# Making the first MLP weight operands during the in-projection: one step per token tile behind its norm, loads behind the projection's weights, sums on VectorE

## The chip, the cores and the metric

One core of one Trainium2 chip runs the kernel. The metric is the device time of one execution in microseconds. The engines are named as in the profile: PE (TensorE, matrix products), PEld (its weight loads), DVE (VectorE), ACT (ScalarE), POOL (GpSimd) and SP (SyncE, which issues almost all the DMAs here).

## The reference

One layer of an encoder with two kinds of attention in parallel, in float32, for 1024 and 256 tokens with the same weights. Cut to what matters here:

```python
n = rms_norm(h, g_mix)
z = n @ w_in                                   # qa, ka, va | qb, kb, vb
qb = axial_rope(rms_norm(qb, g_qnorm))         # per head of 64
kb = axial_rope(rms_norm(kb, g_knorm))
oa = diff_attention(qa, ka, va); ob = gqa_attention(qb, kb, vb)
h = h + concat(oa, ob) @ w_out
h = h + relu(rms_norm(h, g_mlp) @ w_ff1) ** 2 @ w_ff2
h = h + sigmoid(rms_norm(h, g_ple) @ w_gate) * (p @ w_proj)
y = rms_norm(h, g_final)
```

## The kernel before

All 1280 tokens are worked on together, as ten tiles of 128. A float32 product is made of three products of a high and a low part (`hi*hi + hi*lo + lo*hi`), so every operand is split first: ACT copies it to the rounded high part, DVE or POOL subtracts that from the operand to get the low part. The MLP uses a seven-product scheme of the Strassen kind on 2x2 blocks, so its weights are needed as sums and differences of four blocks `a11, a12, a21, a22`, each split, named by numbers 1 to 7.

The program has these stages: in-projection (0 to about 215 us), attention woven with the last projection units and the output projection (to about 800 us), the two MLP products (to about 1600 us), then gate and output.

The in-projection goes by units. A `b_unit` makes 256 columns of q (or k and v) of mixer B: for each token tile 24 matmuls into a PSUM bank `psb`, then `norm_rope`, a chain of small operations that normalises and rotates each head: `sq` (ACT, squares), `zg` and `ss` (DVE, scaled copy and sum of squares), `rq4v` (DVE), `rq4u` and `rr` (ACT, logarithm and exponential), three small `rq4u` steps and `rr` (DVE), `ra` (POOL, twice) beside `rb` (DVE, twice), and at last `ro` (DVE). Two token tiles later PE transposes `ro` into `trb`, ACT and DVE split that into `qkl`, and it is written to DRAM. A `va_unit` makes 256 columns of v: 24 matmuls per tile into `psv`, split into `vl`, written to DRAM as `vad`. `weave` alternates groups of matmuls of two units: units b0 and va1 from about 68 to 140 us, then b1 and `qk_a` (the first q and k of mixer A, banks `psa`, split into `zl`) to about 206 us. PSUM banks and the tiles `vl`, `w1o` and `xt` come in pairs.

Beside these units `early_w1` makes the split MLP weights of the first two groups of 256 columns of `w_ff1`: it loads two 512 KB blocks per group into the slots Q0 and Q1 (`w1e`), scales them by `gmlp` on ACT (eight 128x256 operations), makes four sums on POOL (`w1t`, lines 473, 474, 479, 480), splits the seven operands (`w1o`: ACT line 466, DVE line 467) and writes each to DRAM (`wed`, 512 KB). It is a generator; `along` takes one step of it after every fourth group of matmuls of the b unit, that is once per token tile. The slots Q0 and Q1 are used again for the first `kt` and `qt` of the attention, and the two buffers of `w1o` are those of `xt`.

The order of the instructions on each engine is set by a scheduler when the program is built: it takes the code in the order written and moves instructions by its own estimate of times. `tc.issue_after(x)` keeps every instruction of the block behind `x` on x's engine. All loads that go through `load` are chained in the order of the code, on SP's queue. Each engine carries out its instructions strictly in that order, so an instruction that waits holds up everything behind it.

Of the kernel before, what the change touches and what calls it, by code (L numbers as in the profile page):

```python
# [14 lines left out]
F32 = mybir.dt.float32  # L15
F32R = mybir.dt.float32r
F16 = mybir.dt.float16
AF = mybir.ActivationFunctionType
ALU = mybir.AluOpType
# [4 lines left out]
P = 128  # L24
# [16 lines left out]
def f(ap):  # L41
    return ap.bitcast(F32)
# [3 lines left out]
def encoder_kernel(ctx: ExitStack, tc: tile.TileContext, x, xT, pT, w_in, w_out, w_ff1, w_ff2, w_gate, w_proj,  # L46
# [38 lines left out]
    V, S, G, PE = nc.vector, nc.scalar, nc.gpsimd, nc.tensor  # L85
    dma = nc.sync.dma_start
# [3 lines left out]
    def load(*args):  # L90

        with tc.issue_after(chain[-1].ins) if chain else contextlib.nullcontext():
            chain[:] = [dma(*args)]
        return chain[0]
# [65 lines left out]
    RAWB = 6  # L160
    EVERY = 4
    FETCH = ((4, 6), (5, 7), (6, 2), (8, 5))

    def load_w(src, cols, n, rawp, wp, tag, lo_eng, between={}, dma=dma):

        c0 = cols
        hi, lo = [], []
        kn = 512 // n
        kw = {"bufs": WHB} if n == 256 else {}
        for kk in range(KD // kn):  # L170
            if kk in between:
                between[kk]()
            raw = rawp.tile([P, kn, n], F32, tag="raw", name=f"raw{tag}", bufs=RAWB if n == 256 else 2)
            w_dma[:] = [dma(raw, src[kk * kn * P:(kk + 1) * kn * P, c0:c0 + n].rearrange("(k p) c -> p k c", p=P))]
            a = wp.tile([P, kn, n], F32R, tag="wh", name=f"wh{tag}", **kw)
            b = wp.tile([P, kn, n], F32R, tag="wl", name=f"wl{tag}", **kw)
            S.activation(a, raw, AF.Copy)
            lo_eng.tensor_tensor(b, raw, f(a[:]), op=ALU.subtract)
            hi += [a[:, i, :] for i in range(kn)]
            lo += [b[:, i, :] for i in range(kn)]  # L180
        return hi, lo
# [4 lines left out]
    def slot(tag, shape, dt, name):  # L186
        return slot_pool[tag].tile(shape, dt, tag=tag, name=name, bufs=1)
# [25 lines left out]
    def pj(name):  # L213
        return ppj.tile([P, 512], F32, tag="pj", name=name)

    def weave(main, side, ratio, stop=False):


        owed = 0.0
        for c in main:  # L220
            owed += c * ratio
            while owed > 0 and side is not None:
                d = next(side, None)
                if d is None:
                    side = None
                    if stop:
                        return
                    break
                if d == 0.0:
                    break  # L230
                owed -= d
        if side is not None:
            drain(side)

    def drain(gen):
        for _ in gen:
            pass
# [28 lines left out]
    def tok_pairs(w, t):  # L266
        wh, wl = w
        c = slice(t * P, (t + 1) * P)
        pr = []
        for k in range(KD):  # L270
            pr += [(xh[:, k, c], wh[k]), (xh[:, k, c], wl[k]), (xl[:, k, c], wh[k])]
        return pr
# [4 lines left out]
    gq = bp.tile([P, 64], F32, name="gq", bufs=1)  # L277
    gk = bp.tile([P, 64], F32, name="gk", bufs=1)

    def norm_rope(ps, t, nh, g):  # L280
        r1 = rstd1[:, t:t + 1]
        sq = bp.tile([P, 4, 64], F32, tag="sq", name="sq")
        zg = bp.tile([P, 4, 64], F32, tag="zg", name="zg")
        ps3 = ps[:, :nh * 64].rearrange("p (h d) -> p h d", d=64)
        S.activation(sq[:, :nh], ps3, AF.Square, scale=r1)
        V.scalar_tensor_tensor(zg[:, :nh], ps3, r1, g[:, None, :].to_broadcast([P, nh, 64]),
                               op0=ALU.mult, op1=ALU.mult)
        ss = bp.tile([P, 4], F32, tag="ss", name="ss")
        V.tensor_reduce(out=ss[:, :nh], in_=sq[:, :nh], axis=AX.X, op=ALU.add)
        rr = bp.tile([P, 4], F32, tag="rr", name="rr")  # L290
        rsqrt(rr[:, :nh], ss[:, :nh], 1.0 / 64, 1e-6, bp, nh, f"rq{nh}")
        a = bp.tile([P, 4, 64], F32, tag="ra", name="ra")
        b = bp.tile([P, 4, 64], F32, tag="rb", name="rb")
        G.tensor_tensor(a[:, :nh], zg[:, :nh], rc[:, t:t + 1, :].to_broadcast([P, nh, 64]), op=ALU.mult)
        z4 = zg[:, :nh].rearrange("p h (a b e) -> p h a b e", a=2, b=2)
        b4 = b[:, :nh].rearrange("p h (a b e) -> p h a b e", a=2, b=2)
        s4 = rs[:, t, :].rearrange("p (a b e) -> p a b e", a=2, b=2)
        for q in range(2):
            V.tensor_tensor(b4[:, :, :, q, :], z4[:, :, :, 1 - q, :],
                            s4[:, None, :, q, :].to_broadcast([P, nh, 2, 16]), op=ALU.mult)  # L300
        G.tensor_tensor(a[:, :nh], a[:, :nh], b[:, :nh], op=ALU.add)
        o = bp.tile([P, 4, 64], F32, tag="ro", name="ro", bufs=3)
        V.tensor_tensor(o[:, :nh], a[:, :nh], rr[:, :nh, None].to_broadcast([P, nh, 64]), op=ALU.mult)
        return o.rearrange("p h d -> p (h d)")

    def b_unit(u, w, hook=None):
# [55 lines left out]
    def va_unit(u, w):  # L362
        for t in range(NT):
            ps = pj("psv")
            yield from mm_gen(ps[:, :256], tok_pairs(w, t))
            hl = bp.tile([P, 2, 2, P], F32R, tag="vl", name="vl")
            v3 = ps[:, :256].rearrange("p (h d) -> p h d", d=P)
            r1 = rstd1[:, t:t + 1]
            S.activation(hl[:, :, 0, :], v3, AF.Copy, scale=r1)
            V.scalar_tensor_tensor(hl[:, :, 1, :], v3, r1, f(hl[:, :, 0, :]), op0=ALU.mult, op1=ALU.subtract)  # L370
            for j in range(2):
                dma(vad[2 * u + j][t * P:(t + 1) * P], f(hl[:, j]))
# [16 lines left out]
    def qk_a(h):  # L389

        for c, dst, sc in ((512 + P * h, kd[h], 1.0), (P * h, qd[h], -0.125 / SLOPES[h])):
            w = load_w(w_in, c, P, rawp, wp, "a", G, dma=load)
            yield from qk_unit(dst, sc, w)

    def wload(c, between={}, dma=dma):
        return load_w(w_in, c, 256, bp, bp, "p", V, between, dma)
# [27 lines left out]
    w_b0, w_va1 = wload(1536, dma=load), wload(1280, dma=load)  # L424
# [26 lines left out]

    def early_w1():
        for p in range(NEW):
            raws = []
            for kh in range(2):
                raw = slot(f"Q{kh}", [P, 4, 256], F32, "w1e")
                load(raw, w_ff1[kh * 512:kh * 512 + 512, p * 256:(p + 1) * 256].rearrange("(k p) c -> p k c", p=P))
                for k in range(4):
                    S.activation(raw[:, k], raw[:, k], AF.Copy, scale=gmlp[:, 4 * kh + k:4 * kh + k + 1])
                raws.append(raw)  # L460
            a11, a12, a21, a22 = (raws[x][:, :, c * P:c * P + P] for c in range(2) for x in range(2))
            yield

            def out(i, src):
                hl = bp.tile([P, 2, 4, P], F32R, tag="xt", name="w1o", bufs=2)
                S.activation(hl[:, 0], src, AF.Copy)
                V.tensor_tensor(hl[:, 1], src, f(hl[:, 0]), op=ALU.subtract)
                dma(wed[p, i], f(hl[:]))

            out(1, a11)  # L470
            t = bp.tile([P, 2, 4, P], F32, tag="qkl", name="w1t", bufs=1)
            s3, s2 = t[:, 0], t[:, 1]
            G.tensor_tensor(s3, a11, a21, op=ALU.subtract)
            G.tensor_tensor(s2, a22, s3, op=ALU.subtract)
            yield
            for i, src in ((6, s2), (7, s3), (2, a12)):
                out(i, src)
                yield
            G.tensor_tensor(s3, a12, s2, op=ALU.subtract)
            G.tensor_tensor(s2, a21, a22, op=ALU.add)  # L480
            for i, src in ((5, s2), (4, a22), (3, s3)):
                out(i, src)
                yield

    def along(main, side, every):

        for n, c in enumerate(main):
            yield c
            if n % every == every - 1:
                next(side, None)  # L490

    early = early_w1()
    weave(along(b_unit(0, w_b0), early, EVERY), va_unit(1, w_va1), 1.0)
    weave(along(b_unit(1, wload(1792, dma=load)), early, EVERY), qk_a(0), 1.0)
    drain(early)
    bs.close()

# [256 lines left out]
    for h in range(4):  # L754
# [6 lines left out]
        ends = (bl[6], al[4], bl[7]) if h == 3 else (bl[6], bl[7], al[4])  # L761
# [245 lines left out]
    side = side_work()  # L1007
# [182 lines left out]
    for n, c in enumerate(side):  # L1190
        flush()
        for m, i in FETCH:
            if len(op_done) >= m and i not in WN[0]:
# [329 lines left out]
    for ti, t in enumerate(FORD):  # L1523
# [19 lines left out]
        ends = []  # L1543
# [62 lines left out]
        for n0 in range(0, 512 if last else D, 512):  # L1606
            n = slice(n0, n0 + 512)
# [54 lines left out]
```

## Time and profile before

| | |
|---|---|
| median of 3 runs | 1719.1 us (1718.8 to 1721.23) |
| the profiled execution | 1720.6 us; its span from first to last instruction 1718.7 us |
| PE busy | 1669.3 us, 97% of the span, so 49.4 us in which PE had nothing running |
| DVE, ACT, POOL busy | 69%, 51%, 39% |
| DMA | mean 162 GB/s over the span; above 300 GB/s in the first 40 us |
| mean granted TensorE clock | 0.996 of full speed |

A row of the timeline gives start, duration, engine, line, operation and tiles, and in brackets the idle time of the engine just before it and what ended that. A row of the windows gives the busy time of each engine in a stretch, then the granted TensorE clock, the DMA share and GB/s. A row of the waits gives who waited for whom: total in us, times, longest.

### The profile page before, as it was taken

To read this page: it belongs to the slowest core of one execution; us is meant where nothing else is said; L and a number is where in the kernel's file an instruction comes from. 1 tells how busy PE (TensorE), PEld (TensorE's weight loads), DVE (VectorE), ACT (ScalarE), POOL (GpSimd) and SP (SyncE) were. 2 spreads that over 40 slices of the span, in tenths; PEclk is the share of its full clock that TensorE was granted. 3 is DMA by queue.
4 is the path that set the end of the run, shared out by engine and by line. 5 is a ranking of instruction groups with operands and counts; after the bars stand their busy time and mean duration, and the time that the engine had idled before them with its cause. 6 is when DMAs were issued, how large, how long until landed. Compare 5 with 4: busy or idle time off the path is not lost.

```text
span 1718.7 us, 27284 instructions
## 1 busy us (share of the span) xinstructions
PE 1669.3 (97%) x9849; PEld 1490.0 (87%) x9849; DVE 1183.8 (69%) x2107; ACT 868.4 (51%) x1749; POOL 673.4 (39%) x659
## 2 busy tenths in 40 slices
PE   8979999999999999999999999999999999999997
PEld 8979888888878888889999999998888888888886
DVE  7777678878878878668666665665665855355666
ACT  8543268767866667675332333333433333354644
POOL 1153445635754435333556665620433400001441
PEclk9999999999999999999999999999999999999999
DMA  9774493432773534395433343449666456532111
GB/s 311 240 255 154 158 236 111 124 121 87 216 204 110 155 99 124 110 314 193 157 126 137 129 151 123 136 162 386 213 219 200 127 192 201 167 121 69 45 44 50
DMA packets 191867, 278.28 MB, mean 162 GB/s; under 512 B 13674, under 2 KB 121076, under 8 KB 191732
## 3 DMA queue, kind: packets, MB, share of 16 engines
q1 hardware_dynamic: 189988, 271.28, 49.3%
q0 software_dynamic: 1600, 5.24, 1.0%
q8 instruction: 78, 1.28, 0.3%
q14 instruction: 57, 0.47, 0.1%
q10 hardware_dynamic: 144, 0.00, 0.0%
HBM read 182.63 MB, written 88.61 MB: 158 GB/s over the span
## 4 chain that ended last, share of the span: by engine, by line
PE 76%; DVE 8%; DMA 6%; ACT 4%; issue 3%; POOL 2%; SPq 1%; POOLq 0%; ACTq 0%; DVEq 0%
PE psa L242 6%; PE pso L242 5%; PE sc L621 5%; PE av L699 5%; PE tr L675 4%; PE psb L242 2%; PE psg L1553 2%; DMA vad<-vl 1%; DVE pl L686 1%; DMA xt<-in_x 1%; PE psv L242 1%; PE f__16296 L156 1%; PE f__15256 L156 1%; PE f__16638 L156 1%; PE f__15601 L156 1%
## 5 line engine op out<-in xcount | busy, mean ns | idle before, releaser
L1350 ACT ACTIVATE ao<-ar 128x1280 fp32r<-128x1280 f32 x56 | 71.3, 1275 | 189.4 <-PE f__16300 L156 37.8
L621 PE MATMUL sc<-kt,qt 128*128 128x512 f32 (+1 forms) x576 | 156.1, 391 | 7.7 <-ACT p L646 5.0
L686 DVE TENSOR_TENSOR pl<-tr,ph 128x512 fp32r<-128x512 f32 x204 | 138.1, 685 | 33.2 <-ACT ph L681 32.0
L1352 DVE TENSOR_TENSOR ao<-ar,ao 128x1280 fp32r<-128x1280 f32 x56 | 93.3, 1666 | 89.0 <-ACT ao L1350 89.0
L681 ACT ACTIVATE ph<-tr 128x512 fp32r<-128x512 f32 x204 | 120.0, 596 | 56.8 <-PE tr L675 50.0
L242 PE MATMUL pso<-ow,mt 128*128 128x512 f32 x480 | 119.3, 395 | 3.5 <-DVE osq L726 1.3
L675 PE MATMUL tr<-ident,p 128*128 128x128 f32 x768 | 115.6, 273 | 6.4 <-DVE pl L686 5.7
L621 PEld LDWEIGHTS sc<-kt,qt 128*128 128x128 f32 x576 | 98.9, 189 | 26.1 <-ACT p L646 6.5
L1553 PE MATMUL psg<-gw,n 128*128 128x512 f32 (+1 forms) x504 | 115.4, 384 | 0.0
L675 PEld LDWEIGHTS tr<-ident,p 128*128 128x128 f32 x768 | 91.4, 140 | 22.8 <-DVE pl L686 9.2
L1553 PEld LDWEIGHTS psg<-gw,n 128*128 128x128 f32 x504 | 90.8, 188 | 19.5
L1071 POOL TENSOR_SCALAR w1r<-w1r,gmlp 128x256 f32<-128x256 f32 x112 | 79.2, 726 | 69.1 <-DMA w1r<-in_w_ff 48.3
L242 PEld LDWEIGHTS pso<-ow,mt 128*128 128x128 f32 x480 | 87.4, 188 | 21.6 <-DVE osq L726 2.0
L699 PE MATMUL av<-ph,vt 128*128 128x256 f32 x544 | 102.3, 289 | 0.9 <-DVE osq L726 0.4
L660 POOL TENSOR_SCALAR p<-p,rl 128x1024 f32<-128x1024 f32 x64 | 75.1, 1176 | 51.0 <-DVE rl L658 48.4
L1144 ACT ACTIVATE w<-w1s 128x512 fp32r<-128x512 f32 x56 | 35.2, 628 | 116.4 <-POOL w1s L1151 54.4
L638 DVE TENSOR_REDUCE mm<-sc 128x1 f32<-128x1024 f32 (+1 forms) x80 | 84.2, 1056 | 8.8 <-PE sc L621 8.3
L699 PE MATMUL av<-pl,vt 128*128 128x256 f32 x408 | 89.6, 301 | 0.0
L699 PEld LDWEIGHTS av<-ph,vt 128*128 128x128 f32 x544 | 82.3, 190 | 6.3 <-DVE osq L726 1.2
L646 ACT ACTIVATE p<-sc,mm 128x1024 f32<-128x1024 f32 x64 | 71.4, 1115 | 25.5 <-DVE mm L638 16.7
L634 DVE CUSTOM_DVE_ANT_0 p<-sc,dist 128x1024 f32<-128x1024 f32 x64 | 77.6, 1219 | 8.3 <-PE sc L621 4.4
L643 ACT ACTIVATE p<-p,mm 128x1024 f32<-128x1024 f32 x64 | 73.5, 1149 | 18.0 <-DVE mm L634 17.2
(1520 smaller groups left out, 4748.8 us busy)
## 6 DMA issues: line engine op xcount, KB each, us to landing
ar<-ad SPq DMA_DIRECT2D x56, 640.0 KB, 4.1
w2r<-in_w_ff SPq DMA_DIRECT2D x56, 512.0 KB, 4.6
qt<-qd SPq DMA_DIRECT2D x160, 128.0 KB, 3.0
ad<-q SPq DMA_DIRECT2D x64, 320.0 KB, 2.8
ad<-qs SPq DMA_DIRECT2D x48, 320.0 KB, 2.2
w1r<-in_w_ff SPq DMA_DIRECT2D x28, 512.0 KB, 4.4
md<-ml SPq DMA_DIRECT2D x40, 256.0 KB, 2.2
mt<-md SPq DMA_DIRECT2D x20, 512.0 KB, 6.3
```

Of the source, the lines that this page charges most:

```text
L242: PE.matmul(ps, a, b, start=i == 0, stop=i == n - 1)
L621: PE.matmul(ps[:, h0:h0 + n], shared["q"][:, cc, v, i * P:(i + 1) * P], kt[:, s0 + h0:s0 + h0 + n], start=v == 0, stop=v == 1)
L634: V.tensor_tensor_reduce(out=p[:, :sn], in0=ps[:, :sn], in1=dst_t[:, off:off + sn], scale=SLOPES[idx], scalar=3.0e38, op0=ALU.add, op1=ALU ...
L638: V.tensor_reduce(out=st["m", i][:, 0:1], in_=ps[:, :sn], axis=AX.X, op=ALU.max, negate=True)
L660: G.tensor_scalar(p[:, :sn], p[:, :sn], rl[:, 0:1], 1.0, op0=ALU.mult, op1=ALU.mult)
L675: PE.transpose(t[:, jj, i * P:(i + 1) * P], st["ws"][i][:, j * P:(j + 1) * P], ident)
L681: S.activation(ph, st["tr", j2], AF.Copy)
L686: V.tensor_tensor(pl, st["tr", j2], f(st["ph", j2][:]), op=ALU.subtract)
L699: PE.matmul(st["av"][:, :256], x_, y_, start=j2 == 0 and n == 0, stop=j2 == nj - 1 and n == len(pr) - 1)
L1071: G.tensor_scalar(raw[:, k], raw[:, k], gmlp[:, 4 * kh + k:4 * kh + k + 1], 1.0, op0=ALU.mult, op1=ALU.mult)
L1352: V.tensor_tensor(ao[:, 1], a, f(ao[:, 0]), op=ALU.subtract)
L1553: ends[:] = [PE.matmul(ps, a, b, start=m == 0, stop=m == len(pr) - 1)]
```

## The change

Four things are changed in the in-projection, none elsewhere.

- The steps of `early_w1` start later in each unit: none in the first eight groups of matmuls of unit b0 (`SKIP`), none in the first four of b1 (`SKIP2`); before there was a step in every fourth group from the start.
- Each step is kept behind the first (ACT, `sq`) and the last instruction (DVE, `ro`) of the norm that was written last, on those two engines (`rope_ends`).
- Both loads of a group now make a step of their own, and the eight scalings the next one: nine steps per group instead of eight. There are 8 + 9 places for 18 steps, the last step is taken after both units. In the code the loads of the second group now come behind the weights of unit b1 and `qk_a`.
- The four sums of each group (`w1t`) are made on DVE instead of POOL.

```diff
+    SKIP = 8
+    SKIP2 = 4
...
+    rope_ends = []
...
-        S.activation(sq[:, :nh], ps3, AF.Square, scale=r1)
+        ends = [S.activation(sq[:, :nh], ps3, AF.Square, scale=r1)]
...
-        V.tensor_tensor(o[:, :nh], a[:, :nh], rr[:, :nh, None].to_broadcast([P, nh, 64]), op=ALU.mult)
+        rope_ends[:] = ends + [V.tensor_tensor(o[:, :nh], a[:, :nh], rr[:, :nh, None].to_broadcast([P, nh, 64]),
+                                               op=ALU.mult)]
...
-            raws = []
-            for kh in range(2):
-                raw = slot(f"Q{kh}", [P, 4, 256], F32, "w1e")
+            raws = [slot(f"Q{kh}", [P, 4, 256], F32, "w1e") for kh in range(2)]
+            for kh, raw in enumerate(raws):
                 load(raw, w_ff1[kh * 512:kh * 512 + 512, p * 256:(p + 1) * 256].rearrange("(k p) c -> p k c", p=P))
+            a11, a12, a21, a22 = (raws[x][:, :, c * P:c * P + P] for c in range(2) for x in range(2))
+            yield
+            for kh, raw in enumerate(raws):
                 for k in range(4):
                     S.activation(raw[:, k], raw[:, k], AF.Copy, scale=gmlp[:, 4 * kh + k:4 * kh + k + 1])
-                raws.append(raw)
-            a11, a12, a21, a22 = (raws[x][:, :, c * P:c * P + P] for c in range(2) for x in range(2))
             yield
...
-            G.tensor_tensor(s3, a11, a21, op=ALU.subtract)
-            G.tensor_tensor(s2, a22, s3, op=ALU.subtract)
+            V.tensor_tensor(s3, a11, a21, op=ALU.subtract)
+            V.tensor_tensor(s2, a22, s3, op=ALU.subtract)
...
-            G.tensor_tensor(s3, a12, s2, op=ALU.subtract)
-            G.tensor_tensor(s2, a21, a22, op=ALU.add)
+            V.tensor_tensor(s3, a12, s2, op=ALU.subtract)
+            V.tensor_tensor(s2, a21, a22, op=ALU.add)
...
-    def along(main, side, every):
+    def along(main, side, skip, every):
         for n, c in enumerate(main):
             yield c
-            if n % every == every - 1:
-                next(side, None)
+            if n >= skip and n % every == every - 1:
+                with tc.issue_after(rope_ends[0].ins), tc.issue_after(rope_ends[1].ins):
+                    next(side, None)
...
-    weave(along(b_unit(0, w_b0), early, EVERY), va_unit(1, w_va1), 1.0)
-    weave(along(b_unit(1, wload(1792, dma=load)), early, EVERY), qk_a(0), 1.0)
+    weave(along(b_unit(0, w_b0), early, SKIP, EVERY), va_unit(1, w_va1), 1.0)
+    weave(along(b_unit(1, wload(1792, dma=load)), early, SKIP2, EVERY), qk_a(0), 1.0)
```

The order of PE's matmuls stays the same but for a handful of places. On DVE, in unit b0 before, between `rq4v` of a tile (its norm's fifth operation) and `ro` of the same tile there stand splits of the next unit's weights (`wlp`), splits of MLP weights (`w1o`) and the start of the next tile's norm:

```order
L138 TENSOR_SCALAR rq4v<-ss 128x4
L318 TENSOR_TENSOR qkl<-trb,qkl 128x512
L178 TENSOR_TENSOR wlp<-rawp,whp 128x512
L467 TENSOR_TENSOR w1o<-w1t,w1o 128x512
L178 TENSOR_TENSOR wlp<-rawp,whp 128x512
L146 TENSOR_TENSOR rq4u<-rr 128x4
L467 TENSOR_TENSOR w1o<-w1t,w1o 128x512
L286 SCALAR_TENSOR_TENSOR zg<-psb,rstd_95,gq 128x256
L289 TENSOR_REDUCE ss<-sq 128x4
L147 TENSOR_TENSOR rq4u<-rq4u,rq4v 128x4
```

The same place on DVE in the changed kernel, one tile of unit b0 from the start of its norm to its end and the MLP work behind it:

```order
L290 SCALAR_TENSOR_TENSOR zg<-psb,rstd_95,gq 128x256
L293 TENSOR_REDUCE ss<-sq 128x4
L303 TENSOR_TENSOR rb<-zg,cs 128x8x16 x2
L375 SCALAR_TENSOR_TENSOR vl<-psv,rstd_95,vl 128x2x128
L138 TENSOR_SCALAR rq4v<-ss 128x4
L146 TENSOR_TENSOR rq4u<-rr 128x4
L147 TENSOR_TENSOR rq4u<-rq4u,rq4v 128x4
L148 TENSOR_SCALAR rq4u<-rq4u 128x4
L149 TENSOR_TENSOR rr<-rr,rq4u 128x4
L307 TENSOR_TENSOR ro<-ra,rr 128x256
L484 TENSOR_TENSOR w1t<-w1e,w1t 128x512
L485 TENSOR_TENSOR w1t<-w1e 128x512
```

The norm is now in one piece, and `w1o` or `w1t` stand behind `ro`. On ACT, in the changed kernel, the splits of the weights of b1 and of `qk_a` (`whp`, `wha`) stand ahead of the first norm of unit b0, and the eight scalings stand between `sq` and `vl` of its third tile:

```order
L179 ACTIVATE wha<-rawa 128x512 x2
L289 ACTIVATE sq<-psb,rstd_95 128x256
L374 ACTIVATE vl<-psv,rstd_95 128x2x128
L322 ACTIVATE qkl<-trb 128x256
L139 ACTIVATE rq4u<-rq4v 128x4
```

```order
L289 ACTIVATE sq<-psb,rstd_95 128x256
L466 ACTIVATE w1e<-w1e,gmlp 128x256 x8
L374 ACTIVATE vl<-psv,rstd_95 128x2x128
L139 ACTIVATE rq4u<-rq4v 128x4
```

Before, the scalings came in four pieces of four, each as soon as its block could be loaded; the one for the second block of the second group stood ahead of the first `whp` of b1 in the middle of unit b0. On SP, at the end of unit b1, the last MLP operands and the first loads of q for the attention (`qt`, into slot Q1) now stand like this; before, those `qt` were issued in unit b0:

```order
L473 DMA wed1_4_1305<-w1o_2948 128x1024
L782 DMA rawq_3052<-in_w_in 128x4x128
L473 DMA wed1_3_1304<-w1o_3003 128x1024
L554 DMA qt_3166<-qd4_64 64x2x256
L782 DMA rawq_3152<-in_w_in 128x4x128
L554 DMA qt_3166<-qd4_64 64x2x256
L325 DMA qd6_66<-qkl_2978 128x2x512
L325 DMA qd7_67<-qkl_2982 128x2x512
L392 DMA qd0_60<-zl_2998 128x2x256
L554 DMA qt_3166<-qd4_64 64x2x256 x2
```

So `qt` moved from the middle of the in-projection to its end. The number and the sizes of the DMAs are as before.

## The prediction

> **What bounds the kernel now.** I read the page's busy times first, then the windows by stage, then PE's waits in the in-projection, then the timelines around each wait.
>
> ```profile
> PE 1669.3 (97%) x9849; PEld 1490.0 (87%) x9849; DVE 1183.8 (69%) x2107; ACT 868.4 (51%) x1749; POOL 673.4 (39%) x659
> ...
> 86.00:129.00 43.00, 34.06 (x276) 33.42 (x276) 33.55 (x76) 19.23 (x48) 22.72 (x23) 0.93 0.75 254
> 129.00:172.00 43.00, 43.00 (x312) 40.45 (x311) 32.22 (x86) 13.91 (x38) 16.82 (x20) 0.99 0.44 154
> 172.00:215.00 43.00, 43.00 (x271) 38.47 (x271) 25.97 (x67) 12.72 (x32) 19.22 (x21) 1.00 0.48 159
> 215.00:258.00 43.00, 42.88 (x260) 37.52 (x258) 31.71 (x54) 27.46 (x53) 21.25 (x21) 1.00 0.92 235
> ```
>
> PE sets the time: it is busy for 97% of the span, and from 129 to 258 us it misses 0.12 us. The stretch of 86 to 129 us, the second half of units b0 and va1, is the exception: 43.00 - 34.06 = 8.94 us idle, at a mean clock of 0.93. Time taken out there arrives at the end unless a later wait takes it back.
>
> ```profile
> PE trb L325 <- DVE ro L303: 7.6, 2, 6.2
> PE psb L242 <- DVE vbl L350: 2.6, 1, 2.6
> PE psb L242 <- DVE zg L286: 1.3, 1, 1.3
> ...
> 106.33 0.44 PE L325 MATMUL trb<-ident,ro 128*128 128x128 f32 x2 [1.45 <-DVE ro L303]
> 112.21 0.38 PE L325 MATMUL trb<-ident,ro 128*128 128x128 f32 x2
> 113.91 0.39 PE L242 MATMUL psb<-whp,xh 128*128 128x256 f32 x1 [1.32 <-DVE zg L286]
> 125.97 0.69 PE L325 MATMUL trb<-ident,ro 128*128 128x128 f32 x2 [6.17 <-DVE ro L303]
> ```
>
> The 8.94 us are three waits, 1.45 + 1.32 + 6.17, all for the norm of a token tile on DVE. Between the first two transposes PE had no wait, so a tile of both units takes 112.21 - 106.33 = 5.88 us.
>
> ```profile
> 68.53:70.00 1.47, 1.47 (x6) 1.35 (x7) 0.93 (x4) 0.94 (x4) 0.12 (x1) 0.50 1.04 331
> 70.00:72.00 2.00, 2.00 (x12) 2.00 (x11) 0.59 (x1) 2.00 (x8) 0.00 (x0) 0.53 0.53 172
> 114.00:116.00 2.00, 2.00 (x17) 2.00 (x18) 2.00 (x7) 1.35 (x4) 1.41 (x2) 1.00 1.08 364
> 126.00:128.00 2.00, 2.00 (x10) 2.00 (x11) 1.91 (x7) 0.96 (x2) 0.73 (x1) 0.50 1.03 238
> 128.00:130.00 2.00, 2.00 (x11) 2.00 (x11) 2.00 (x6) 0.82 (x3) 0.85 (x2) 0.52 0.65 171
> 130.00:132.00 2.00, 2.00 (x20) 2.00 (x18) 1.93 (x4) 0.00 (x0) 1.73 (x1) 1.00 0.94 373
> ```
>
> A long wait costs more than itself. After the 6.17 us the granted clock is 0.50 and 0.52 for four microseconds: 21 matmuls instead of the 40 that fit at the rate of the last row (20 in 2 us), a loss of 19 x 0.1 = 1.9 us. After the 2.6 us wait for `vbl` (it ended at 68.53) it is 0.50 and 0.53, a loss of 0.74 + 0.94 = 1.7 us. After 1.32 us the clock stays at 1.00.
>
> The Trainium skill, TensorE: Matmul & The Clock Gate, section "Why this matters for your kernels", puts the limit higher: no gaps of PE over about 3 us. By that rule the 2.6 us wait would have cost no clock; the rows show that here it did, so the measurement decides what a wait left over would cost.
>
> Why the norm was late:
>
> ```profile
> 100.49 1.71 ACT L459 ACTIVATE w1e<-w1e,gmlp 128x256 f32<-128x256 f32 x4 [2.72 <-DMA w1e<-in_w_ff]
> 102.85 0.69 DVE L467 TENSOR_TENSOR w1o<-w1e,w1o 128x512 fp32r<-128x512 f32 x1 [2.76 <-ACT w1o L466]
> 109.84 1.71 ACT L459 ACTIVATE w1e<-w1e,gmlp 128x256 f32<-128x256 f32 x4 [2.08 <-DMA w1e<-in_w_ff]
> 112.10 1.36 DVE L178 TENSOR_TENSOR wlp<-rawp,whp 128x512 fp32r<-128x512 f32 x1 [2.27 <-ACT whp L177]
> ...
> 107.13 0.15 DVE L138 TENSOR_SCALAR rq4v<-ss 128x4 f32<-128x4 f32 x1
> 118.25 1.25 DVE L146 TENSOR_TENSOR rq4u<-rr 128x4 f32<-128x4 f32 x1
> 123.49 1.22 DVE L138 TENSOR_SCALAR rq4v<-ss 128x4 f32<-128x4 f32 x1
> 125.49 0.42 DVE L303 TENSOR_TENSOR ro<-ra,rr 128x256 f32<-128x256 f32 x1
> ...
> 123.39 1.30 POOL L480 TENSOR_TENSOR w1t<-w1e 128x512 f32<-128x512 f32 x1
> ```
>
> Two things are to be seen. First, queues: ACT stood 2.72 and 2.08 us before the scalings, until the second group's weights landed; DVE, with a `w1o` and a `wlp` at its head, stood 2.76 and 2.27 us for ACT; behind these stood `zg` and the rest of a norm. Second, DVE and POOL: `rq4v`, 0.15 us at 107.13, takes 1.22 us at 123.49 and ends with POOL's sum; `rq4u` at 118.25 loses 1.10 us in the same way.
>
> **The change part by part.**
>
> *Steps behind the norm, later start.* In the changed order a tile's norm stands in one piece on DVE, and the `w1o` or `w1t` behind its `ro`. A clean norm:
>
> ```profile
> 139.01 0.47 ACT L285 ACTIVATE sq<-psb,rstd 128x256 f32<-128x256 f32 x1 [1.29 <-PE psb L242]
> 144.04 0.43 DVE L303 TENSOR_TENSOR ro<-ra,rr 128x256 f32<-128x256 f32 x1
> ```
>
> From `sq` to the end of `ro` that is 144.47 - 139.01 = 5.5 us. PE transposes a tile two tiles later: `sq` starts about 5.3 us into a tile (75.52, below, less 68.53 and the 1.7 us of slow clock), the transposes come 3 x 5.88 = 17.6 us into it, so the norm may take 12.3 us; 6.8 us are free. All three waits go: -8.94 us, and the slow clock, -1.9 us.
>
> *Loads behind the projection's weights.* The second group's `w1e` no longer stand ahead of `whp` on ACT; that is part of the waits counted. The reverse cost: `wha` now stands on ACT ahead of the first `sq` of b0, so ACT waits there for `rawa`.
>
> ```profile
> DMA to landing us min/median/max: 3.0/5.0/6.1
> ...
> 69.48 0.79 SPq L372 DMA_DIRECT2D vad<-vl  x2
> 75.52 0.47 ACT L285 ACTIVATE sq<-psb,rstd 128x256 f32<-128x256 f32 x1 [0.84 <-PE psb L242]
> ```
>
> The first row is `rawa`'s. In the new order six issues more, about 0.5 us each, lie ahead of the second `rawa`, so it goes out near 72.5 and lands by 77.5 (median) or 78.6 (longest); with two ACT operations of 0.6 us `sq` starts 2 to 4 us after 75.52. Unit b0 starts at 68.53; its third tile needs the bank of the first after two tiles and the 1.7 us of slow clock, at 68.53 + 11.76 + 1.7 = 82.0, and `sq` and `zg` take 1 us, so an `sq` before 81 costs nothing. I take 0; the bounds are 0 and, if the landing slips by another 3 us, 2 us.
>
> *The step of eight scalings.* Two rows of 1.71 us: 3.4 us on ACT between `sq` and `vl` of the third tile. From `sq` to the `psv` matmuls that need the bank again it is 5.88 x 2 + 0.7 - 5.3 = 7.2 us; 0.5 + 3.4 + 0.5 (`vl` on ACT) + 0.5 (on DVE) = 4.9. Hidden; without that cover at most the 3.4 us.
>
> *Sums on DVE.*
>
> ```profile
> L467 DVE TENSOR_TENSOR w1o<-w1t,w1o x8: 678/685/692, 90.7 to 138.3; 128x512 fp32r<-128x512 f32 x8
> L473 POOL TENSOR_TENSOR w1t<-w1e x2: 1295/1304/1312, 86.7 to 104.7; 128x512 f32<-128x512 f32 x2
> ```
>
> POOL loses 8 x 1.30 = 10.4 us. DVE has no such sum in the trace; the nearest row, `w1o`'s subtraction of the same shape, has 0.685 us, so DVE gains 8 x 0.685 = 5.5 us (bounds: nothing, as it no longer waits for POOL in eight places, up to 1.1 us each; 10.4, if DVE were as slow as POOL). DVE's busy time from 129 to 172 is 32.22 of 43 us; two sums and a split, 2.1 us, in a tile of 5.88 us leave the norm its place, and 6.8 us of slack take up the rest. 0 on the path.
>
> The Trainium skill speaks against this part: Perfetto Trace Analysis, section "Optimizing Scalar/DVE Operations", says that the two engines share an SBUF port, "so offloading operations between those two might not help". The rows above agree that they block each other; by that rule the second cause of the waits would stay, in the other direction. It is the second rival below.
>
> *q for the attention, later.* `qt` now stands behind the last two `wed` on SP.
>
> ```profile
> 197.71 0.42 DVE L303 TENSOR_TENSOR ro<-ra,rr 128x256 f32<-128x256 f32 x1
> 212.54 0.86 PE L621 MATMUL sc<-kt,qt 128*128 128x512 f32 x3
> ...
> qt<-qd SPq DMA_DIRECT2D x20, 128.0 KB, 7.8
> ...
> DMA to landing us min/median/max: 4.0/6.4/13.5
> ```
>
> On the clock of the trace of before: the ninth tile's `ro` ends at 198.1, two splits behind it (1.4 us) make 199.5, then ten issues of about 0.5 us, some behind `zl`: the last `qt` goes out near 205. It needs 7.8 us (median from 195 to 260 us, where DMA is full), so it lands near 212.8, and the first scores start at 212.54: between -4 and +0.3 us, taken as 0; with the longest landing of a `kt` (13.5, the last row) it would be a wait of 6 us.
>
> *Sum.* -8.94 - 1.9 = -10.8 us. The wait for `vbl` at 68.5 lies ahead of everything moved and stays. Against the profiled execution, 1720.6 (span 1718.7), that is 1709.8 (span 1707.9); that execution lies 1.5 us above the median, so for the median 1719.1 - 10.8 = 1708.3.
>
> **The rivals.**
>
> 1. *Part of the waits comes back in the same units*: ACT at `rawa`, or the scalings, make PE wait once. One wait of 2.6 us with its clock, 2.6 + 1.7 = 4.3 us, gives 1712.6. For it: ACT now waits for two loads ahead of the norm. Against: the slack counted above.
>
> 2. *The sums block as much from DVE as from POOL.* Then `rq4u` and `rq4v` of the long wait keep their 1.10 + 1.07 = 2.2 us, as POOL's `ra` waits for DVE's sums, and with the clock of a 2.6 us wait at most 1.7: up to 3.9 us stay, 1712.2. Against: the norm has 6.8 us to spare, so a block of 2 us would not reach PE.
>
> 3. *Slower: `qt` comes too late.* The first scores wait and everything behind them. The gain is eaten when that wait with its clock loss reaches 10.8 us: 8.9 us, a landing at 221.4, 16.4 us after its issue; at 20 us it is 12.5 + 1.9 - 10.8 = 3.6 us slower, 1722.7. For it: the DMA share is 0.92 from 215 to 258, and `wed` adds 1 MB just before. Against: the longest landing is 13.5 us.
>
> 4. *No effect*: new waits as long as the old ones, the norm bound by something else than the queues, 1719. Against: behind 129 us, with fewer steps, the same norm keeps PE without a wait.
>
> **How the numbers follow.** Chances: the sum as it stands, 0.62; rivals 1 and 2 together, 0.22; rival 4, 0.08; rival 3, 0.06; more than the sum (a wait or slow clock outside these rows goes too), 0.02. The prediction is 1708.3. The range takes in the first two cases and their spread: 1.45 us less than counted on the good side, 1706.5; rival 1 with a second wait of 1.3 us, 1714.0. A measurement of this kernel tells 0.2%, 3.4 us, from no change. Faster (below 1715.7): 0.62 + 0.22 + 0.02, less 0.01 for the tail of rival 1: 0.85. Same: 0.08, that 0.01 and 0.01 of rival 3, where its wait only cancels the gain: 0.10. Slower: 0.05.
>
> **What would show it.** Right: from 76 to 130 us PE without a wait, clock 1.00; on DVE no 1.2 us in a 128x4 operation beside a sum; the first scores near 201.7. Wrong: an `sq` of b0's first tile after 80 us with a PE wait for `zg` behind it; PE waiting for `trb` in a tile with two sums; a wait of the first scores for a DMA.

## The result, and the profile after

| kernel | median | against before, same chip | profiled execution (span) |
|---|---|---|---|
| before | 1718.95 us (1718.67 to 1721.23) | | 1720.6 us (1718.7) |
| after | 1710.49 us (1708.09 to 1711.18) | 0.9945 [0.9928, 0.9963] | 1710.98 us (1708.7) |

The change makes the kernel 8.5 us faster; 10.8 us were forecast. The page after, and the windows of the four stretches that the prediction showed (PE, PEld, DVE, ACT, POOL, then clock, DMA share, GB/s):

```profile
PE 1667.9 (98%) x9849; PEld 1489.0 (87%) x9849; DVE 1178.4 (69%) x2115; ACT 868.2 (51%) x1749; POOL 663.4 (39%) x651
...
86.00:129.00 43.00, 43.00 (x359) 42.46 (x358) 34.67 (x96) 14.91 (x40) 10.30 (x14) 1.00 0.53 185
129.00:172.00 43.00, 43.00 (x294) 39.33 (x293) 34.11 (x92) 17.96 (x48) 20.17 (x23) 1.00 0.50 184
172.00:215.00 43.00, 39.38 (x221) 33.79 (x220) 24.26 (x50) 16.75 (x34) 20.77 (x19) 0.99 0.90 249
215.00:258.00 43.00, 42.24 (x256) 37.78 (x257) 32.91 (x60) 29.92 (x59) 18.59 (x20) 0.93 0.71 176
```

The hole of 8.94 us from 86 to 129 us is closed, at full clock. A new one stands in the third row: 43.00 - 39.38 = 3.62 us, and the clock of the fourth is 0.93. PE's waits over the whole span and the timeline at the new hole, then its windows:

```profile
PE psb L156 <- ACT xh L256: 4.9, 1, 4.9
PE sc L627 <- ACT p L652: 4.6, 6, 1.9
PE sc L627 <- DMA qt<-qd: 3.6, 1, 3.6
```

```profile
215.01 2.05 PE L627 MATMUL sc<-kt,qt 128*128 128x512 f32 x4 [3.62 <-DMA qt<-qd]
```

```profile
213.00:215.00 2.00, 0.00 (x0) 0.02 (x1) 0.00 (x0) 0.28 (x1) 2.00 (x2) 0.81 1.11 232
215.00:217.00 2.00, 1.99 (x5) 1.61 (x6) 0.00 (x0) 0.00 (x0) 0.13 (x1) 0.50 1.09 346
217.00:219.00 2.00, 2.00 (x12) 2.00 (x11) 1.23 (x3) 0.63 (x2) 0.00 (x0) 0.50 1.14 189
...
221.00:223.00 2.00, 2.00 (x15) 1.83 (x15) 1.23 (x3) 0.00 (x0) 0.00 (x0) 0.98 1.02 355
```

The waits for `trb`, `zg` and `vbl` are gone from the list. The first scores of mixer A wait 3.62 us for their `qt`, and six microseconds at clock 0.50 follow.

Since PE's order is almost the same in both kernels, equal matmuls can be laid side by side. How much earlier PE is after the change than before:

| place | before us | after us | earlier by |
|---|---|---|---|
| a `psv` of the first units | 42.59 | 41.45 | 1.1 |
| `psb` behind the former `vbl` wait and its slow clock | 71.93 | 66.46 | 5.5 |
| `psb` behind the three waits | 129.23 | 112.69 | 16.5 |
| a `psa` ahead of the attention | 207.62 | 190.62 | 17.0 |
| first scores of mixer A | 228.12 | 215.01 | 13.1 |
| the first matmul behind the slow clock, an `sc` | 231.34 | 221.10 | 10.2 |
| end of the span | 1718.7 | 1708.7 | 10.0 |

So three things happened: 5.5 us at the start, which the sum did not hold; 11.5 us (17.00 - 5.47) in the units, against 10.8 forecast; and 6.8 us (17.00 - 10.23) given back at mixer A's `qt`, forecast as 0. The experiments ask what the first and the last of these are, and which part of the change brought the 11.5. "In the units" is meant in this way below: how much more PE is ahead of the kernel before at that `psa` (207.62) than at the first `psb` of the table (71.93).

### The profile page after: what moved, and what is told of

Its sections match the earlier page's. It is cut to its first block, busy times and chain, and to the rows that moved or that the text cites. A ratio compares the mean times of both kernels' runs of the same rounds, so it can differ in the third digit from the quotient of the medians.

```text
span 1708.7 us, 27274 instructions
## 1 busy us (share of the span) xinstructions
PE 1667.9 (98%) x9849; PEld 1489.0 (87%) x9849; DVE 1178.4 (69%) x2115; ACT 868.2 (51%) x1749; POOL 663.4 (39%) x651
## 4 chain that ended last, share of the span: by engine, by line
PE 77%; DVE 9%; issue 4%; ACT 4%; DMA 3%; POOL 3%; SPq 1%; POOLq 0%; DVEq 0%; ACTq 0%
PE sc L627 5%; PE av L705 5%; PE psa L244 4%; PE pso L244 4%; PE psb L244 4%; PE tr L681 4%; PE psv L244 3%; PE psg L1559 2%; DVE pl L692 1%; DVE nlo L1184 1%; PE f__16296 L156 1%; PE f__15256 L156 1%; PE f__16638 L156 1%; PE f__15601 L156 1%; PE f__15938 L156 1%
```

## The experiments

Each was timed in five rounds beside the kernel before; the times of before were 1719.4, 1719.12 and 1718.7 us (medians of 11, 18 and 10 runs) in the three groups 1 to 4, 5 to 8 and 9 to 11.

**1. The changed kernel again**, unaltered.

> The changed kernel once more, unaltered. In the profiled execution of it the wait for `vbl` at 68.5 (2.6 us and 1.7 us of slow clock) was gone too, though nothing that stands ahead of it was changed, and a new wait of 3.62 us for `qt` stood at 211.4. Theory: the first is a matter of the execution (the loads of the start land some us earlier or later), the second belongs to the change. Then this trace has a `vbl` wait between 0 and 2.6 us at about 66, and again a `qt` wait of 3 to 4 us before the first scores of mixer A, whatever the start does; time 1710.5 +- 1.5. Rival: the `qt` wait is there only because the start was early and PE ran ahead of the DMAs; then a trace with the `vbl` wait has no `qt` wait, and one with the `qt` wait has no `vbl` wait.

Measured: 1711.94 us, 0.9965 [0.9952, 0.9978].

```profile
PE sc L627 <- DMA qt<-qd: 4.3, 1, 4.3
PE psa L244 <- DVE o L753: 0.6, 1, 0.6
PE psb L244 <- DVE vbl L355: 0.3, 1, 0.3
```

In PE's waits from 20 to 262 us the `qt` wait is back, with 4.3 us; the `vbl` wait is 0.3. In the profiles of the eleven experiments PE's wait for `vbl` is 0.3, 1.9, 0.7, 1.2, none, 0.8, none, none, 1.1, 0.6 and 0.7 us (the two with `lam` moved, 7 and 8, have none), against 2.6 before and none after, and the code ahead of it is the same in all but those two. It belongs to the execution and not to the change. The rival is not settled by this run alone, as neither trace of the changed kernel has a long `vbl` wait; run 2 takes it up.

**2. The sums back on POOL.**

```diff
-            V.tensor_tensor(s3, a11, a21, op=ALU.subtract)
+            G.tensor_tensor(s3, a11, a21, op=ALU.subtract)
```
(and the other three sums alike; also three sums of the MLP, `qs` on lines 1292, 1294 and 1298, went from DVE to POOL)

> The changed kernel with the eight sums back on POOL. Theory: the three waits of 86 to 129 us came from the order of the queues, and a norm has 6.8 us to spare; DVE may wait 1.1 us for POOL in some 128x4 operations, and no PE wait comes of it: 1710.5 within 1.5 us. Rival: the block between POOL and DVE was what made the norm late; then at least one PE wait for `ro` or `zg` comes back between 76 and 190 us, 1.5 to 4 us with its slow clock: 1712 to 1714.5.

Measured: 1708.84 us, 0.9942 [0.993, 0.9954]. PE's waits from 20 to 262 us, then a row of DVE's and one of POOL's timeline:

```profile
PE psb L244 <- DVE vbl L355: 1.9, 1, 1.9
PE sc L627 <- issue: 1.3, 1, 1.3
PE psa L244 <- DVE o L753: 0.6, 1, 0.6
...
89.52 1.25 DVE L146 TENSOR_TENSOR rq4u<-rr 128x4 f32<-128x4 f32 x1
...
89.45 1.31 POOL L479 TENSOR_TENSOR w1t<-w1e,w1t 128x512 f32<-128x512 f32 x1
```

DVE is blocked beside POOL's sums as before (1.25 us; the median of this operation is 0.177), and no wait of PE comes of it: the norm has the time. That is the theory. The MLP's sums play no part: PE is 11.7 us ahead of before at 262 us and 11.3 at the end. The kernel is even 3.1 us faster than in run 1 (1.7 than the first measurement of the change). The trace gives a reason outside the units: mixer A's scores wait 1.3 us instead of 4.3, and no slow clock follows. The trace puts this wait down to nothing in particular, but the third of mixer A's four `qt`, issued at 208.55, landed 7.6 us later, 0.2 us before the scores began at 216.39. Here PE came 3 to 4 us later, from a `vbl` wait of 1.9 us with slow clock, and mixer B's four `qt` went out in one piece (table below). So what the start loses can be hidden by a late `qt`, and the rival of run 1 has this much truth; but `qt` is late in this trace too.

**3. Steps one token tile earlier.**

```diff
-    SKIP = 8
-    SKIP2 = 4
+    SKIP = 4
+    SKIP2 = 0
```

> The changed kernel with the steps starting one token tile earlier in each unit (SKIP 4, SKIP2 0), so that all 18 steps fit beside the units. Theory: mixer A's first `qt` is late since the last `wed` and the `qt` of mixer B, which wait for slots Q0 and Q1, are issued close before it and fill SP's queue and the DMA engines; issued 6 to 12 us earlier they are out of the way: the wait of 3.62 us falls below 1.5 us and the slow clock behind it goes: 1705 to 1708. Rival: the wait comes from PE being ahead of transfers that hang on the end of unit b1; then it stays at 3 to 4 us and the time at 1710.5. Against both: a step one tile earlier stands before the weights of the next units have landed on ACT, and a PE wait for `zg` in the first tiles of b0 costs 1 to 3 us.

Measured: 1706.94 us, 0.9928 [0.9916, 0.994], 3.6 us faster than the first measurement of the change and 5.0 us than run 1. No `qt` wait, no slow clock between 8 and 1697 us; from 20 to 262 us PE waits 1.5 + 0.7 + 0.6 us, the first two at the start. The theory holds as far as it goes; it leaves open whether the last `wed` or mixer B's `qt` matter, as both are earlier here.

**4. No place behind the norm.**

```diff
-                with tc.issue_after(rope_ends[0].ins), tc.issue_after(rope_ends[1].ins):
-                    next(side, None)
+                next(side, None)
```

> The changed kernel without keeping a step behind the last norm (no issue_after in `along`); later start, separate loads and sums on DVE stay. The scheduler then draws the steps forward: the last `wed` is issued some 20 rows of SP earlier. Theory: the place behind `ro` is what keeps the norm in one piece; without it `w1o` stands inside a norm again and one or two waits for `trb` or `zg` of 1 to 3 us come back between 86 and 190 us, while the `qt` wait of 3.62 us goes, as the transfers are out of the way: 1707 to 1712. Rival: the loads behind the projection's weights alone took the waits away; then no PE wait between 76 and 190 us, no `qt` wait, 1705.

Measured: 1711.32 us, 0.9959 [0.9947, 0.9971].

```profile
PE trb L330 <- DVE ro L307: 2.8, 3, 1.5
...
PE psb L244 <- DVE zg L290: 0.3, 1, 0.3
```

As forecast: 3.1 us of waits for the norm are back, none longer than 1.5 us and none followed by slow clock, and the `qt` wait is gone, since the scheduler drew the steps forward. The two nearly cancel. In the units PE gains 7.0 us here, against 11.5 with the place behind the norm, so the place is worth about 4.5 of the 11.5 us, somewhat more than the waits.

**5. Fewer bytes of the second group.**

```diff
-                dma(wed[p, i], f(hl[:]))
+                if p:
+                    dma(sink[i], f(hl[:, 1, 0]))
+                else:
+                    dma(wed[p, i], f(hl[:]))
```

(`sink` is a small tile that nobody reads; the MLP takes the first group's operands in place of the second's, so this kernel leaves out a part of the layer and only its time means something.)

> The changed kernel, in which the second group's seven operands are made as before, but only 64 KB of each 512 KB is written, to tiles that nobody reads; the MLP takes the first group's operands for both groups. Number and place of the issues stay, 3.1 MB of 3.7 MB are not moved. Theory: mixer A's first `qt` is late because these bytes crowd the DMA engines just before; then the wait of 3.6 to 4.3 us falls below 1.5 us, without slow clock: 1705 to 1708. Rival: the place of the issues on SP counts, mixer B's first `qt` behind the last `wed` and all else behind them; then the wait stays at 3 to 4.5 us and the time at 1710 to 1712.

Measured: 1711.75 us, 0.9953 [0.994, 0.9965]. The theory of the bytes falls. The row of PE's timeline at mixer A's first scores:

```profile
217.03 1.66 PE L634 MATMUL sc<-kt,qt 128*128 128x512 f32 x4 [2.62 <-ACT zl L823]
```

The wait stands at the same matmul, 2.62 us, with 3.1 MB less to move. The trace puts it down to `zl` on ACT, which ended 0.06 us before. More likely it is the same wait: the third of mixer A's four `qt`, issued at 208.90, landed 7.9 us later, 0.2 us before the scores. In the changed kernel and in run 1 that `qt` (issued at 207.16 and 207.84, landed 7.6 and 8.1 us later) also lands 0.2 to 0.3 us before them, and in runs 2 and 9 the scores begin before the same `zl` is done. Mixer B's `qt` went out at 188.2 to 193.6 us in this run, as late as in the changed kernel.

**6. The kernel before with the sums on DVE** (the four lines of `w1t` as in run 2, the other way round; also the four sums of the MLP's later weights, `w1s` on lines 1150, 1151, 1160 and 1161, went to DVE).

> The kernel before with the eight sums on DVE and nothing else. Theory: the three waits of 86 to 129 us came from the order of the queues, the block by POOL added little; they stay at 6 to 9 us in all, and the time at 1716.5 to 1719.5. Rival: the block by POOL made the norm of the long wait late (1.10 and 1.07 us); then the 6.17 us fall by 2 us or more and the time by 2 to 4 us: 1715 to 1717.

Measured: 1715.06 us, 0.9974 [0.9964, 0.9985].

```profile
PE trb L325 <- DVE ro L303: 3.9, 2, 2.3
PE psb L242 <- DVE zg L286: 1.5, 2, 0.9
```

The rival holds: 4.1 us faster in the median, and the longest wait falls from 6.2 to 2.3 us. The sums of the MLP have no part in it: PE is 6.7 us ahead of before at 207 us and 6.7 at the end. But in this trace 4.75 of the 6.7 us are there before the units begin, where this run changes nothing, and the units gain only 1.9 us, since five waits of 0.7 to 2.3 us are left there. What the median has beyond these 1.9 us stays open. In the order of before, where a norm stands in pieces, the block by POOL was a cause of the long wait; with the norm in one piece (run 2) it is none.

**7. The kernel before with `lam` later** (its load stays in place, into another tile).

```diff
-    lam_p = ...; lam_e = ...; neglam = ...
     weave(along(b_unit(0, w_b0), early, EVERY), va_unit(1, w_va1), 1.0)
+    lam_p = ...; lam_e = ...; neglam = ...
     weave(along(b_unit(1, wload(1792, dma=load)), early, EVERY), qk_a(0), 1.0)
```

> The kernel before, with the four operations on `lam` behind units b0 and va1 instead of ahead of them (the load stays in its place, into another tile). Theory: the wait for `vbl` at 66 to 68 us stands in most executions of every kernel with 0 to 2.6 us, as DVE waits for `lam_t` ahead of `vbl`, and its length goes with the landing times of the execution; without it PE waits there for less than 1 us and the time falls by 1.5 to 4.3 us: 1715 to 1718. Rival: later waits, or the loads of w_b0, take up what is won: 1719 +- 0.8.

Measured: 1718.19 us, 0.9993 [0.9984, 1.0001]. The `vbl` wait is gone, and in the trace PE is 3.7 us ahead of the one of before at 74 us and ends 3.4 us earlier (span 1715.3); the median falls by 0.9 us, which is not told from nothing. So the start of the profiled execution of before was probably a long one, and most executions lose less there. By this run about 1 us of the 5.5 at the start is to be expected in a comparison of medians.

**8. Steps one tile earlier, `lam` and `gsub` later** (the edits of 3 and 7 together, and the scaling of `gsub` moved along).

> The changed kernel with the steps one tile earlier (as in the run before, 1706.9) and the operations on `lam` and the scaling of `gsub` moved behind units b0 and va1. Theory: both waits, for `vbl` at 66 us and for `qt` at 211 us, are gone in one execution: 1703 to 1705.5, with less than 0.8 us of PE wait between 60 and 215 us. Rival: when PE arrives earlier, the transfers of mixer A's first `kt` and `qt` are late again: a `qt` wait of 1 to 3 us, 1705.5 to 1707.5.

Measured: 1707.14 us, 0.9927 [0.9915, 0.9939]. The trace is as the theory says, with no `qt` wait, and 0.7 us for `trb` and 0.6 for `psa` as PE's only waits from 20 to 262 us, span 1703.6; the median misses the theory's range and lies in that of the rival, whose `qt` wait is not there. Run 3, with the start as it was, has 1706.94: with no `qt` wait the start decides little.

**9. Operands 4 and 5 exchanged.** Operand 4 is the last that reads slot Q1, which mixer B's `qt` waits for.

```diff
-            for i, src in ((5, s2), (4, a22), (3, s3)):
+            for i, src in ((4, a22), (5, s2), (3, s3)):
```

> The changed kernel with two operands exchanged in the order of each group: 4 (a22) ahead of 5, so that the slot Q1 is free one step earlier. Bytes and number of steps stay, the last two `wed` stay where they were; mixer B's first `qt` goes ahead of them on SP, some 6 us earlier. Theory, after the run with few bytes: the wait at 211 us comes from the place of mixer B's first `qt`, close ahead of the last `qd` of unit b1, which hold back `dist` and with it `kt` and `qt` of mixer A; then `dist` is issued 2 us sooner after the last `trb`, the wait falls below 1.5 us, without slow clock: 1706 to 1709. Rival: the late `wed` do it; then the wait stays at 2.5 to 4.5 us: 1710 to 1712.

Measured: 1706.24 us, 0.9929 [0.9917, 0.9942]: 5.7 us faster than run 1, and 4.3 us than the first measurement of the change. PE's waits from 20 to 262 us:

```profile
PE psb L244 <- DVE vbl L355: 1.1, 1, 1.1
PE psa L244 <- DVE o L753: 0.6, 1, 0.6
PE psv L244 <- DVE vl L375: 0.5, 1, 0.5
```

SP's timeline, first of the changed kernel, then of this one:

```profile
183.56 0.79 SPq L473 DMA_DIRECT2D wed<-w1o  x1
184.40 0.63 SPq L554 DMA_DIRECT2D qt<-qd  x1
...
189.09 2.23 SPq L554 DMA_DIRECT2D qt<-qd  x2
191.41 0.54 SPq L818 DMA_DIRECT2D kd<-zl  x1
193.17 1.60 SPq L325 DMA_DIRECT2D qd<-qkl  x2
194.83 0.46 SPq L1014 DMA_DIRECT2D dist<-in_dist  x1
197.10 0.36 SPq L818 DMA_DIRECT2D kd<-zl  x1
197.55 0.43 SPq L544 DMA_DIRECT2D vt<-vbd  x1
198.03 1.13 SPq L538 DMA_DIRECT2D kt<-kd  x1
...
202.99 6.40 SPq L554 DMA_DIRECT2D qt<-qd  x4
```

```profile
178.95 2.58 SPq L554 DMA_DIRECT2D qt<-qd  x4
182.57 0.34 SPq L473 DMA_DIRECT2D wed<-w1o  x1
...
185.48 0.33 SPq L473 DMA_DIRECT2D wed<-w1o  x1
...
194.00 2.00 SPq L325 DMA_DIRECT2D qd<-qkl  x2
196.05 0.50 SPq L1014 DMA_DIRECT2D dist<-in_dist  x1
196.65 0.41 SPq L544 DMA_DIRECT2D vt<-vbd  x1
197.11 0.76 SPq L538 DMA_DIRECT2D kt<-kd  x1
199.01 0.36 SPq L818 DMA_DIRECT2D kd<-zl  x1
...
205.17 3.67 SPq L554 DMA_DIRECT2D qt<-qd  x3
```

Same bytes, same steps, the last two `wed` at about the same time; mixer B's `qt` moved ahead of them, and the wait went. In the first list these four issues run from 184.4 to 191.3 us between the last `wed` and the last `qd`. The rest of SP's queue stands behind them: the last `qd`, `dist`, `kt`, and mixer A's `qt`. Laid out for eight traces, times from the start of unit b1's last `trb` (runs 4, 6, 7, 10 and 11 are like the first three rows: `dist` at +2.1, A's last `qt` at +13.1 to +14.8, no wait):

| trace | mixer B's last `qt` issued | `dist` issued | mixer A's last `qt` issued | wait of A's scores |
|---|---|---|---|---|
| before | -64.7 | +2.1 | +14.9 | 0 |
| 3 (early) | -17.6 | +2.1 | +14.6 | 0 |
| 8 (early, lam) | -17.7 | +2.1 | +15.1 | 0 |
| 9 (4 before 5) | -11.7 | +3.4 | +15.6 | 0 |
| 2 (sums on POOL) | -4.1 | +3.3 | +16.5 | 1.3 |
| 5 (fewer bytes) | +0.4 | +3.9 | +17.2 | 2.6 |
| after | 0.0 | +4.3 | +18.3 | 3.6 |
| 1 (again) | -0.1 | +4.5 | +19.0 | 4.3 |

From about +16 on, every microsecond by which A's last `qt` goes out later is about one of waiting. The exchange of operands takes 2.7 to 3.4 us off this time and with it the whole wait.

Two more things moved with it. `dist` comes only 0.9 to 1.1 us sooner, not the 2 us expected; the rest arises behind it, where the scheduler changed SP's order too. In the changed kernel the `kd` at 197.10, which waited 1.7 us for POOL's `zl`, stands ahead of `vt` and the first `kt`; in run 9 and in all other kernels here it stands behind that `kt`. Runs 2 and 5 have this `kd` behind the `kt` and wait 1.3 and 2.6 us all the same, so B's late `qt` is enough for a wait. But of the 1 to 2 us that run 5 saves, it is open how much is the bytes and how much the `kd`. And PE came to this place 3 us later than in the first trace of the changed kernel, which by run 2 shortens the wait as well. That the place of B's `qt` does it and not the start rests on run 8 (no wait, with PE only 1 us later) and on the times: four of run 9's five lie below all ten of the changed kernel.

**10. The later start alone**, in the kernel before.

```diff
-            if n % every == every - 1:
+            if n >= skip and n % every == every - 1:
```
(with `SKIP` 8 and `SKIP2` 4, as in the change)

> The kernel before with the later start of the steps alone (none in the first 8 and 4 places), which also puts the second group's loads behind the weights of b1; sums on POOL, loads and scalings in one step, no place behind the norm. Theory: the late second group on ACT and DVE is one of several causes of the three waits (7.4 us in all in the run with sums on DVE alone it was 5.4); alone it takes out a half: PE waits of 3 to 6 us between 76 and 190 us, no `qt` wait: 1712 to 1716. Rival: the later start alone does it all, and the other parts are not needed: less than 2 us of waits, 1707 to 1710.

Measured: 1713.1 us, 0.9969 [0.9957, 0.9981].

```profile
PE trb L327 <- DVE ro L305: 4.3, 3, 2.2
```

As the theory said: about half. The later start alone brings 5.6 us in the median. In the units of the traces it brings 4.4 us, the sums on DVE alone 1.9 us (run 6), and the place behind the norm 4.5 us (run 4): 10.8 of the 11.5 us. Whether the parts simply add up was not tried in pairs, nor the loads as a step of their own. There is no `qt` wait: without `issue_after` mixer B's `qt` are issued from 128 us on.

**11. Steps one tile earlier, sums on POOL** (the edits of 3 and 2 together, the MLP's three sums included).

> The changed kernel with the steps one tile earlier and the sums on POOL. Theory: with the norm in one piece behind which each step stands, the engine of the sums makes no difference: no PE wait for `ro` or `zg` of more than 1 us and 1706.9 +- 1.0, as with the sums on DVE. Rival: POOL's sums, one tile earlier beside the weights' splits of the next units, block the norm: waits of 1 to 3 us and 1708 to 1711.

Measured: 1706.5 us, 0.9928 [0.9916, 0.9941], PE's waits from 20 to 262 us 0.7, 0.6 and 0.2 us, none of them for `ro` or `zg`. The engine of the sums makes no difference once the steps are behind the norm. Runs 3, 8, 9 and 11 lie within 1 us of each other and are not told apart. Each is 3.4 to 5.7 us below the changed kernel, which is clear of the noise against run 1 but not against the first measurement, whose interval overlaps theirs; 9 does it with one line.

## Why the prediction was right, and where it was not

- *The three waits, -8.94 - 1.9.* Right: none is left, the clock is 1.00 from 86 to 172 us, and PE gains 11.5 us in the units, 0.7 more than the sum had. The two causes named, the queues and the block by POOL, both take part: the queues with 4.4 and 4.5 us (runs 10 and 4), the block with 1.9 (run 6). One row was read wrongly: the `rq4u` at 118.25 does not stand beside a sum but beside a weight split of POOL, which the change leaves there; only the 1.07 us at 123.49 were a sum's.

```profile
117.89 1.59 POOL L178 TENSOR_TENSOR wla<-rawa,wha 128x512 fp32r<-128x512 f32 x1 [1.99 <-ACT wha L177]
```

- *`qt` for the attention, "taken as 0 (between -4 and +0.3 us)".* This is the step that failed. The transfers that were costed did come in time: mixer B's first scores start without a wait,

```profile
195.66 0.86 PE L627 MATMUL sc<-kt,qt 128*128 128x512 f32 x3
```

  and earlier than the forecast 201.7, by the 5.5 us of the start and about half a microsecond. But only their own landing was costed, not what stands behind them on SP. These are mixer A's `kt` and `qt`, which have 16 us between the last `trb` and the last issue, and got 18.3. Measured: 3.9 us at the scores and 2.9 us of slow clock, 6.8 us; a "wait of 6 us" was in the text, for another transfer and another reason. In the medians it is 4.3 to 5.7 us (run 9).
- *Rival 3* named this wait and gave it 0.06 for the case that it eats the gain. In the trace it came at 6.8 of those 10.8 us, for mixer A's `qt` and not for mixer B's, which rival 3 priced; so it took away a part of the gain and not the whole.
- *"The wait for `vbl` ... stays".* It is 2.6 us in one trace and nothing in another of kernels that are equal up to there. A wait that ends with a first load is not a constant; the profiled execution of before was one of the long ones. In the profiled pair this term, 5.5 us, covers most of the one missed at `qt`.
- *`wha` and `rawa` ahead of the first norm, 0.* Right, but closer than it looks: `sq` of b0's first tile starts at 73.93, and PE is 5.5 us earlier here, so on the clock of before this is 79.4. That is 3.9 us later than before, within the 2 to 4 forecast, and 1.6 us short of the 81 from which it would cost. No PE wait follows.

```profile
73.39 0.63 ACT L179 ACTIVATE wha<-rawa 128x512 fp32r<-128x512 f32 x1 [1.22 <-DMA rawa<-in_w_in]
73.93 0.46 ACT L289 ACTIVATE sq<-psb,rstd 128x256 f32<-128x256 f32 x1
```

- *Scalings, hidden.* Right: no PE wait from 76 to 211 us.
- *Sums on DVE, 0 on the path.* Right for the changed order, and 0.685 us for one was right (685 ns, next row; where POOL's splits of weights stand beside it one took 1.67). The rule of the Trainium skill (Perfetto Trace Analysis, "Optimizing Scalar/DVE Operations") that such a move might not help is borne out in the changed order, where the sums are as good on POOL (runs 2 and 11); in the order of before the trace disagrees, with 1.9 us in the units (run 6).

```profile
L478 DVE TENSOR_TENSOR w1t<-w1e x2: 685/686/686, 92.5 to 152.3; 128x512 f32<-128x512 f32 x2
```

The forecast of 1708.3 lies 2.2 us from the 1710.5 measured, and that is in part luck: in the profiled pair the span forecast, 1707.9, is met within 0.8 us only because 5.5 us at the start and 0.7 us in the units, neither of them in the sum, stand against the 6.8 us missed at `qt`. With the term that failed taken out by an exchange of two operands, the kernel comes to 1706.2, 12.5 us below before: the 10.8 of the sum, 0.7 more in the units, and 1 us that stays open; it is about what run 7 gives for the start.

## What to carry to other kernels

When a transfer is moved to a later place of an in-order queue, cost everything that stands behind it there and not only its own landing: here the moved `qt` was in time, and the next unit's was not. A slot that is shared hands the lateness of one use to the next, so put the operation that frees it first; an exchange of two operands was worth 4 to 6 us. And before a wait near the start of a profile is counted as fixed, look at a second execution.

## What the runs showed of the hardware

The record of PE's granted clock, as start, length (us) and clock, of the trace after, of run 2 (up to 449 us) and of run 10, without the half clock at the end of the span:

```
after    9.4  204.80  1.0 |  214.2   6.83  0.5 |  221.1 1481.38  1.0
run 2    9.1   58.03  1.0 |   67.1   3.41  0.5 |   70.5  378.88  1.0
run 10  10.2  443.73  1.0 |  453.9   3.41  0.5 |  457.4 1249.28  1.0
```

These lengths are all multiples of 3.413 us: 1 and 2, 17, 60, 111, 130, 366 and 434 of them. Waits of 3.62, 4.3 and 6.2 us were each followed by two such stretches at half clock, waits of 1.94, 2.27, 2.6 and 2.62 by one. The 2.18 us of run 10 (a `trb` at 116.87) was followed by none, nor was any of 1.6 us or less in these units. Later, in the attention, a wait of 1.65 us in run 1 (ended at 451.77) was followed by one stretch, and one of 1.93 us in the changed kernel (ended at 450.96) by none. So it is not the length alone that decides.

```profile
66.61 0.36 PE L244 MATMUL psb<-whp,xh 128*128 128x256 f32 x1 [1.94 <-DVE vbl L355]
...
116.87 0.44 PE L327 MATMUL trb<-ident,ro 128*128 128x128 f32 x2 [2.18 <-DVE ro L305]
```

The Trainium skill, TensorE: Matmul & The Clock Gate, section "The HAM clock gate", tells of a window of 3413 ns that runs freely, and of half clock after at least one idle window. The lengths agree with the window; a gap of 1.94 us that was enough, and one of 2.18 that was not, fit a window that begins where it will, but not that it must be wholly idle.
